# A fifth channel tile of a Conformer convolution moves from TensorE to taps on ScalarE and GpSimd

## The chip, the cores and the metric

The kernel runs on one core of a Trainium2 chip. The metric is the device time of one execution in microseconds. Times come from repeated runs; engine times, waits and order come from one profiled execution.

## The reference

A decoder trunk of two layers over 512 positions of 1024 channels. Layer 0 mixes tokens with a gated DeltaNet, layer 1 with a Conformer convolution; each layer then attends to a fixed memory and applies a squared-ReLU MLP. The change lies in the Conformer module:

```python
def conformer_conv(h, w_pw1, b_pw1, w_dw, b_dw, ln_g, ln_b, w_pw2, b_pw2):
    u = h @ w_pw1 + b_pw1
    u = u[..., :D_MODEL] * jax.nn.sigmoid(u[..., D_MODEL:])
    c = causal_depthwise_conv(u, w_dw) + b_dw       # width 31
    c = jax.nn.silu(layer_norm(c, ln_g, ln_b))      # over the channels
    return c @ w_pw2 + b_pw2
```

Everything is float32. A full-precision product is made of three matmuls of split operands (high by high, low by high, high by low).

## The kernel before

Activations lie channel by position: eight tiles of 128 channels x 512 positions. A weight half of 128 x 1024 is loaded by SP's queue (`raw`), ScalarE casts it to the high part (`wh`, L207), and VectorE or GpSimd subtracts to get the low part (`wl`, L70 by way of the helper `tt`); three halves are held ahead (`NW = 3`). For the first pointwise weight GpSimd makes all low parts, for layer 1's K and V weights every second one. Instructions are written in one order; a planner then orders each engine's queue by what is ready in its own costs, so that the order on an engine can differ from the written one.

The Conformer (`conformer`) walks through 32 positions (`CONV_SEQ`): 0 to 15 are pointwise products (two for each channel tile: value and gate, `pw_mm`, 24 matmuls each), 16 to 31 are the K and V products of the next cross-attention (`kv_unit(1, u)`), which need nothing of the Conformer and fill TensorE. The evacuation `pw_ev(m)` of tile m waits for both products and for `norm.rb`, the row scale that `norm.stat` and `norm.spread` make: VectorE scales the gate (`sg`) and the value (`pa`), ScalarE applies the sigmoid, and VectorE multiplies the two (`x` or `glu`).

Positions are held in four phases (position 4t + s stands in block s). Two ways of convolving follow:

- Tiles 0 to 3 (`m < NDVE`) by taps: `dve_conv` gives a list of 31 taps; the first is a ScalarE product into PSUM (`ca`, L1038), the other 30 are VectorE multiply-adds on that PSUM tile (L73), and ScalarE copies the end to SBUF (L1044). `taps_dve` puts some of the waiting taps into the written order after each position, `TAP_RATE` per microsecond given. `turn(m)` (`"d"` in `CONV_AFTER`) then transposes the tile on TensorE (`cvT`, L1055), so that positions become rows.
- Tiles 4 to 7 on TensorE: 16 DMAs regroup the tile (`xg`), nine DMAs bring its matrices of taps (`taps(m)`, `"t"`), and `conv(m, js)` (`"c"`) makes 72 matmuls whose output already has positions as rows (`cv`, L1071 and L1074).

Either way four VectorE additions per tile add the row block to `Y`, into which the convolution's bias had been loaded, and four `bn_stats` take its statistics. When all eight tiles are in, `ln()` (`"l"`) normalises `Y` (eight VectorE instructions, L79), and `ln_out(m)` (`"o"`) transposes each channel tile back (`lnT`, L1102), applies scale, bias and SiLU on ScalarE and splits the result (`lsh`, `lsl`) for the second pointwise weight. `CONV_AFTER` sets by hand after which position each of these steps is written. All SBUF tiles of 128 x 512 come out of one set of 69 slots; PSUM has eight tiles.

The first layer's short convolutions use both forms as well: `conv_taps` makes a product on ScalarE (`cvq`, L458) and adds it on GpSimd (`cva`, L70) for the first of its taps where it is told to.

Of the kernel before, what the change touches and what calls it, by code (L numbers as in the profile page):

```python
# [21 lines left out]
_VECS = ["dn_norm", "cv_norm", "xa_norm0", "xa_norm1", "xa_mem0", "xa_mem1", "mlp_norm0", "mlp_norm1",  # L22
         "ln_g", "ln_b", "b_pw2"]
OFF = {n: 8 * i for i, n in enumerate(_VECS)}
# [5 lines left out]
OFF["w_tap"] = _o  # L30
_o += NDVE * 31
OFF["out_norm"] = _o
# [6 lines left out]
def tile_trunk(ctx, tc, xT, memT, prm_d, adt_d, bdw_d, tap_d, fin_d, w_ab, w_kq, w_v, w_z, w_dno, w_pw1, w_pw2,  # L39
# [41 lines left out]
    def c4(t):  # L81
        return t.rearrange("p (c i) -> p c i", c=4)
# [901 lines left out]
    def taps(m):  # L984

        TAPS[m] = []
        for i in range(9):
            t = slot(s="tap")
            nc.sync.dma_start(out=t, in_=tap_d[m - NDVE, i])
            TAPS[m].append(t)  # L990

    def conformer(norm, hres, nxt):
# [4 lines left out]
        for y in Y:  # L997
            for i in range(2):
                nc.sync.dma_start(out=y[i], in_=bdw_d[i * 512:(i + 1) * 512].partition_broadcast(P))

# [4 lines left out]
        def pw_ev(m):  # L1005
# [4 lines left out]
            tt(dve, a, st.pop((m, 0)), norm.rb, ALU.mult)  # L1010
            if m < NDVE:
                x7 = fsp.tile([P, 1024], F32, tag="fs", name=nm("x7"))[:, 0:1008].rearrange("p (q t) -> p q t", q=7)
                pool.memset(x7[:, :, 0:10], 0.0)
                stt(x7[:, 3:7, 8:136], c4(a), pc("b_pw1", m), c4(sg), ALU.add, ALU.mult)
                act.copy(x7[:, 0:3, 9:137], x7[:, 4:7, 8:136])
                todo.extend(dve_conv(m, x7))
                return
# [10 lines left out]

        todo, acc = [], {}

        def dve_conv(m, x7):

            def tap(d):
                w, u, e = pc("w_tap", m * 31 + 30 - d), d // 4, d % 4
                src = x7[:, 3 - e:7 - e, 8 - u:136 - u]
                if d == 0:
                    st["ca"] = psum("ca")
                    act.activation(c4(st["ca"]), src, AF.Copy, scale=w)  # L1038
# [13 lines left out]
        def turn(m):  # L1052
# [4 lines left out]
            for r in range(4):  # L1057
                y = Y[r][m // 4][:, m % 4 * P:m % 4 * P + P]
                tt(dve, y, ps[:, r * P:(r + 1) * P], y, ALU.add)
                dve.bn_stats(out=bn[:, (r * 8 + m) * 6:(r * 8 + m) * 6 + 6], in_=y)  # L1060
# [221 lines left out]
    h = xattn(0, n1, h, n2)  # L1282
    n3 = Norm("cv_norm", deng=pool)
    h = mlp(0, n2, h, n3, lambda: (mem_gain(1, 0), mem_gain(1, 1), taps(NDVE)))
    n4 = Norm("xa_norm1")
# [14 lines left out]
    def finish(hid, cur):  # L1300
# [3 lines left out]
        for c, g in LAST:  # L1304
# [14 lines left out]
            if g == 0:  # L1319
# [69 lines left out]
def _taps(np, w):  # L1389
# [11 lines left out]
    e = np.concatenate([e[:, :, :, 0:8].reshape(128, 8, 128), e[:, :, :, 8].reshape(128, 8, 16)], axis=2)  # L1401
    e = e.reshape(4, 32, 8, 9, 16)[:, :, NDVE:]
    t = np.zeros((8 - NDVE, 9, 4, 32, 16, 32), w.dtype)
    for c in range(32):
        t[:, :, :, c, :, c] = e[:, c].transpose(1, 2, 0, 3)
    return t.reshape(8 - NDVE, 9, 128, 512)


def _layout(np, i):
# [3 lines left out]
    def vec(v):  # L1413
# [6 lines left out]
            i["xa_mem_norm"][1], i["mlp_norm"][0], i["mlp_norm"][1], i["cv_ln_g"][0],  # L1420
            i["cv_ln_b"][0], i["cv_b_pw2"][0], i["cv_b_pw1"][0]]
    cols = [vec(v) for v in vecs]
    cols.append(i["dn_w_conv"][0].T.reshape(24, 128, 4).transpose(1, 0, 2).reshape(128, 96))
    cols.append(i["cv_w_dw"][0].T.reshape(8, 128, 31)[:NDVE].transpose(1, 0, 2).reshape(128, NDVE * 31))
    cols.append(i["dn_out_norm"][0].reshape(128, 1))
# [39 lines left out]
```

## Time and profile before

| | |
|---|---|
| runs (three) | 1562.58, 1564.87, 1565.54 us; median 1564.87 |
| profiled execution | 1567.44 us, span 1565.7 us, mean granted clock 0.987 |
| Conformer, first pointwise matmul to second pointwise weight | 868.5 to 1046.8 us of the span |

Engines are PE (TensorE), PEld (its weight loads), DVE (VectorE), ACT (ScalarE), POOL (GpSimd) and SP (the DMA queue). A row of the timeline has the start and length in us, the engine, the line, the operation and the tiles as output<-input; in square brackets stands how long the engine had been idle and what released it. A group has the count, its busy time, the mean of one in ns and the idle time before them. A stretch has its bounds, its length, the busy time and count of each engine, the granted share of TensorE's clock, and the DMA engines' share and GB/s. Matmuls overlap: one of 512 columns is shown as 0.39 us, while the next one starts 0.23 us after it.

### The profile page before, as it was taken

What the parts mean: (1) busy time and instruction counts of PE and PEld (TensorE: products, weight loads), DVE (VectorE), ACT (ScalarE), POOL (GpSimd) and SP (SyncE); (2) the same over time, 40 slices, a digit from 0 to 9 for tenths busy, and PEclk for the clock granted to TensorE, in tenths of its full rate; (3) what the DMA queues carried; (4) which work ended last, traced back from release to release, by engine and by line L of the source; (5) the groups of instructions that cost most, each with busy time, mean ns of one, the idle gap of its engine ahead of it and who ended that gap; (6) DMA issues with size and microseconds to landing.
All of it is one profiled execution on the core that took longest, in us unless ns stands there. A gap on an engine that the chain in (4) does not pass through costs nothing.

```text
span 1565.7 us, 19421 instructions
## 1 busy us (share of the span) xinstructions
PE 1530.1 (98%) x7630; PEld 1289.4 (82%) x7630; DVE 903.2 (58%) x1372; ACT 653.3 (42%) x1017; POOL 186.6 (12%) x202
## 2 busy tenths in 40 slices
PE   8999996999999999999999999999999999999998
PEld 6887885988888888888888889978888888888886
DVE  6798788666655444343435499874545443434441
ACT  5855656454544443231424332264434442323332
POOL 1221122101212000000002441112112000000000
PEclk9999998899999999999999999999999999999999
DMA  5222122252222222233224624443213223322231
GB/s 169 66 81 68 55 68 87 85 179 75 87 68 68 94 95 94 96 104 97 95 94 154 207 87 152 167 137 106 69 40 108 94 95 95 102 99 95 94 108 54
DMA packets 51115, 156.17 MB, mean 100 GB/s; under 512 B 6608, under 2 KB 8912, under 8 KB 51024
## 3 DMA queue, kind: packets, MB, share of 16 engines
q1 hardware_dynamic: 51024, 154.93, 30.4%
q8 instruction: 60, 0.98, 0.3%
q14 instruction: 31, 0.25, 0.0%
HBM read 151.76 MB, written 2.10 MB: 98 GB/s over the span
## 4 chain that ended last, share of the span: by engine, by line
PE 89%; DVE 6%; ACT 1%; issue 1%; DMA 1%; SPq 1%; POOL 0%; ACTq 0%; POOLq 0%; DVEq 0%
PE up L229 7%; PE up L230 7%; PE up L231 7%; PE dn L230 6%; PE dn L229 6%; PE dn L231 6%; PE pw L229 3%; PE pw L231 3%; PE pw L230 3%; PE q L229 2%; PE xo L230 2%; PE q L230 2%; PE xo L231 2%; PE q L231 2%; PE xo L229 2%; PE h L230 1%
## 5 line engine op out<-in xcount | busy, mean ns | idle before, releaser
L207 ACT CAST wh<-raw 128x1024 fp32r<-128x1024 f32 x248 | 260.3, 1051 | 675.3 <-PE dn L230 194.8
L70 DVE TENSOR_TENSOR wl<-raw,wh 128x1024 fp32r<-128x1024 f32 x224 | 277.4, 1239 | 96.5 <-ACT wh L207 94.9
L229 PE MATMUL up<-xh,wh 128*128 128x512 f32 x512 | 200.3, 391 | 0.0
L231 PE MATMUL up<-xh,wl 128*128 128x512 f32 x512 | 199.3, 389 | 0.0
L230 PE MATMUL up<-xl,wh 128*128 128x512 f32 x512 | 199.3, 389 | 0.0
L231 PE MATMUL dn<-uh,wl 128*128 128x512 f32 x448 | 174.4, 389 | 0.0
L230 PE MATMUL dn<-ul,wh 128*128 128x512 f32 x448 | 174.4, 389 | 0.0
L229 PE MATMUL dn<-uh,wh 128*128 128x512 f32 x448 | 174.4, 389 | 0.0
L70 DVE TENSOR_TENSOR h<-dn,h 128x512 f32<-128x512 f32 x56 | 41.8, 747 | 163.3 <-PE dn L231 163.3
L73 DVE SCALAR_TENSOR_TENSOR rl<-up,rb 128x512 f32<-128x512 f32 x64 | 44.2, 690 | 157.0 <-PE up L231 157.0
L229 PEld LDWEIGHTS up<-xh,wh 128*128 128x128 f32 x512 | 96.1, 188 | 20.3 <-issue 0.5
L230 PEld LDWEIGHTS up<-xl,wh 128*128 128x128 f32 x512 | 96.2, 188 | 20.2 <-issue 0.5
L231 PEld LDWEIGHTS up<-xh,wl 128*128 128x128 f32 x512 | 96.1, 188 | 20.0
L70 POOL TENSOR_TENSOR sq<-sq,sq 128x512 f32<-128x512 f32 x30 | 47.8, 1592 | 465.0 <-ACT sq L304 465.0
L229 PEld LDWEIGHTS dn<-uh,wh 128*128 128x128 f32 x448 | 84.1, 188 | 17.5
L231 PEld LDWEIGHTS dn<-uh,wl 128*128 128x128 f32 x448 | 84.1, 188 | 17.4
L230 PEld LDWEIGHTS dn<-ul,wh 128*128 128x128 f32 x448 | 84.1, 188 | 17.4
L73 DVE SCALAR_TENSOR_TENSOR ca<-x,prm,ca 128x512 f32<-128x512 f32 x120 | 87.8, 748 | 3.0 <-ACT ca L1038 1.2
L229 PE MATMUL h<-xh,wh 128*128 128x512 f32 x192 | 78.7, 410 | 3.1 <-ACT xh L297 3.1
L230 PE MATMUL h<-xl,wh 128*128 128x512 f32 x192 | 76.5, 398 | 0.6 <-DVE xl L73 0.6
L231 PE MATMUL h<-xh,wl 128*128 128x512 f32 x192 | 76.1, 397 | 0.0
L70 POOL TENSOR_TENSOR wl<-raw,wh 128x1024 fp32r<-128x1024 f32 x24 | 57.6, 2407 | 114.5 <-ACT wh L207 107.4
(334 smaller groups left out, 3034.3 us busy)
## 6 DMA issues: line engine op xcount, KB each, us to landing
raw<-w_up SPq DMA_DIRECT2D x64, 512.0 KB, 3.6
raw<-w_dn SPq DMA_DIRECT2D x64, 512.0 KB, 3.6
raw<-w_pw SPq DMA_DIRECT2D x24, 512.0 KB, 3.7
tap<-tap SPq DMA_DIRECT2D x36, 256.0 KB, 5.4
raw<-w_kq SPq DMA_DIRECT2D x16, 512.0 KB, 3.6
raw<-w_k SPq DMA_DIRECT2D x16, 512.0 KB, 3.8
raw<-w_vv SPq DMA_DIRECT2D x16, 512.0 KB, 3.7
raw<-w_q SPq DMA_DIRECT2D x16, 512.0 KB, 3.6
```

The costliest lines, as they stand in the source:

```text
L70: return e.tensor_tensor(out=o, in0=a, in1=b, op=op)
L73: dve.scalar_tensor_tensor(out=o, in0=a, scalar=s, in1=b, op0=op0, op1=op1)
L207: ins = [act.copy(h, raw)]
L229: pe.matmul(ps, wh, xh, start=first, stop=False)
L230: pe.matmul(ps, wh, xl, start=False, stop=False)
L231: pe.matmul(ps, wl, xh, start=False, stop=last)
```

## The change

Tile 4 is no longer convolved by TensorE, and five tiles (`NTAP = 5`) go by taps. Tiles 1 to 4 keep `dve_conv`. Tile 0 goes by a new function, `pool_conv`: ScalarE makes each tap's product in SBUF (in two pieces where the tap crosses a phase) and GpSimd adds it to the sum; `taps_pool` places two taps per pointwise position, one per K or V position, and three after a convolution. The bias enters with the first tap (Identity with a bias in place of Copy), so a turned tile is not added to `Y`: ScalarE copies the transposed block to `Y` and VectorE takes its statistics straight from PSUM. Only the half of `Y` for tiles 4 to 7 is still loaded with the bias. The row scale is spread after the second product in place of the third, its diagonal is made by VectorE instead of GpSimd, and tile 0 is evacuated there. The steps of `CONV_AFTER` are placed anew: the matrices of tiles 6 and 7 are loaded after positions 3 and 13, and tile 0 is turned after position 20.

```diff
-NDVE = 4
+NTAP = 5
...
         for y in Y:
-            for i in range(2):
-                nc.sync.dma_start(out=y[i], in_=bdw_d[i * 512:(i + 1) * 512].partition_broadcast(P))
+            nc.sync.dma_start(out=y[1], in_=bdw_d[512:1024].partition_broadcast(P))
...
-            if m < NDVE:
+            if m == 0:
+                x4 = c4(wp.tile([P, 544], F32, tag="cv", name=nm("xp"), bufs=NCV))
+                pool.memset(x4[:, :, 0:8], 0.0)
+                stt(x4[:, :, 8:136], c4(a), pc("b_pw1", m), c4(sg), ALU.add, ALU.mult)
+                todo_p.extend(pool_conv(m, x4))
+                return
+            if m < NTAP:
...
+        def pool_conv(m, x4):
+            a = acc[m] = slot(s="ca")
+
+            def tap(d):
+                w, u, e = pc("w_tap", m * 31 + 30 - d), d // 4, d % 4
+                if d == 0:
+                    act.activation(c4(a), x4[:, :, 8:136], AF.Identity, scale=w, bias=pc("b_dw", m))
+                    return
+                b = slot(s="cvp")
+                act.activation(c4(b)[:, e:4], x4[:, 0:4 - e, 8 - u:136 - u], AF.Copy, scale=w)
+                if e:
+                    act.activation(c4(b)[:, 0:e], x4[:, 4 - e:4, 7 - u:135 - u], AF.Copy, scale=w)
+                tt(pool, a, a, b, ALU.add)
+
+            return [lambda d=d: tap(d) for d in range(31)]
...
-                    act.activation(c4(st["ca"]), src, AF.Copy, scale=w)
+                    act.activation(c4(st["ca"]), src, AF.Identity, scale=w, bias=pc("b_dw", m))
...
+        def taps_pool(n):
+            for _ in range(min(len(todo_p), n)):
+                todo_p.pop(0)()
...
-                y = Y[r][m // 4][:, m % 4 * P:m % 4 * P + P]
-                tt(dve, y, ps[:, r * P:(r + 1) * P], y, ALU.add)
+                y = ps[:, r * P:(r + 1) * P]
+                act.copy(Y[r][m // 4][:, m % 4 * P:m % 4 * P + P], y)
                 dve.bn_stats(out=bn[:, (r * 8 + m) * 6:(r * 8 + m) * 6 + 6], in_=y)
...
-                if (m, hf) == (1, 0):
+                if (m, hf) == (0, 1):
                     norm.spread()
-                    pw_ev(0)
-                if hf == 1 and m > 0:
+                if hf == 1:
                     pw_ev(m)
...
             taps_dve(5.4 if kind == "p" else 2.8)
+            taps_pool(2 if kind == "p" else 1)
...
                 taps_dve({"c": 2.0 * len(js)}.get(what, 0.0))
+                taps_pool(3 if what == "c" else 0)
...
-    n3 = Norm("cv_norm", deng=pool)
+    n3 = Norm("cv_norm")
...
-CONV_AFTER = [(3, ("t", 5)), (11, ("d", 0)), (12, ("c", 4, 0, 1)), (13, ("c", 4, 2, 3)), (13, ("t", 6)),
-              (14, ("c", 5, 0, 1, 2, 3)), (14, ("t", 7)), (15, ("d", 1)), (16, ("c", 6, 0, 1, 2, 3)), (18, ("d", 2)),
-              (18, ("c", 7, 0, 1, 2, 3)), (23, ("d", 3)), (23, ("l", 0))]
+CONV_AFTER = [(3, ("t", 6)), (9, ("d", 1)), (13, ("d", 2)), (13, ("c", 5, 0, 1, 2, 3)), (13, ("t", 7)),
+              (16, ("c", 6, 0, 1, 2, 3)), (17, ("d", 3)), (18, ("c", 7, 0, 1, 2, 3)), (20, ("d", 0)), (23, ("d", 4)),
+              (23, ("l", 0))]
```

The host side packs the convolution's bias and the fifth tile's taps into the parameter tile, and the tap matrices of three tiles instead of four.

More of the change, by code (lines that the diff above doesn't have):

```diff
@@ L22 @@
 _VECS = ["dn_norm", "cv_norm", "xa_norm0", "xa_norm1", "xa_mem0", "xa_mem1", "mlp_norm0", "mlp_norm1",
-         "ln_g", "ln_b", "b_pw2"]
+         "ln_g", "ln_b", "b_pw2", "b_dw"]
 OFF = {n: 8 * i for i, n in enumerate(_VECS)}
@@ L30 @@
 OFF["w_tap"] = _o
-_o += NDVE * 31
+_o += NTAP * 31
 OFF["out_norm"] = _o
@@ L988, in taps @@
             t = slot(s="tap")
-            nc.sync.dma_start(out=t, in_=tap_d[m - NDVE, i])
+            nc.sync.dma_start(out=t, in_=tap_d[m - NTAP, i])
             TAPS[m].append(t)
@@ L1027, in pw_ev @@
             xg[m] = x4
-        todo, acc = [], {}
+        todo, todo_p, acc = [], [], {}
+        def pool_conv(m, x4):
[11 more added lines that the diff above has]
+            return [lambda d=d: tap(d) for d in range(31)]
         def dve_conv(m, x7):
@@ L1282, in tile_trunk @@
     h = xattn(0, n1, h, n2)
-    n3 = Norm("cv_norm", deng=pool)
-    h = mlp(0, n2, h, n3, lambda: (mem_gain(1, 0), mem_gain(1, 1), taps(NDVE)))
+    n3 = Norm("cv_norm")
+    h = mlp(0, n2, h, n3, lambda: (mem_gain(1, 0), mem_gain(1, 1), taps(NTAP)))
     n4 = Norm("xa_norm1")
@@ L1401, in _taps @@
     e = np.concatenate([e[:, :, :, 0:8].reshape(128, 8, 128), e[:, :, :, 8].reshape(128, 8, 16)], axis=2)
-    e = e.reshape(4, 32, 8, 9, 16)[:, :, NDVE:]
-    t = np.zeros((8 - NDVE, 9, 4, 32, 16, 32), w.dtype)
+    e = e.reshape(4, 32, 8, 9, 16)[:, :, NTAP:]
+    t = np.zeros((8 - NTAP, 9, 4, 32, 16, 32), w.dtype)
     for c in range(32):
         t[:, :, :, c, :, c] = e[:, c].transpose(1, 2, 0, 3)
-    return t.reshape(8 - NDVE, 9, 128, 512)
+    return t.reshape(8 - NTAP, 9, 128, 512)
 def _layout(np, i):
@@ L1420, in _layout @@
             i["xa_mem_norm"][1], i["mlp_norm"][0], i["mlp_norm"][1], i["cv_ln_g"][0],
-            i["cv_ln_b"][0], i["cv_b_pw2"][0], i["cv_b_pw1"][0]]
+            i["cv_ln_b"][0], i["cv_b_pw2"][0], i["cv_b_dw"][0], i["cv_b_pw1"][0]]
     cols = [vec(v) for v in vecs]
     cols.append(i["dn_w_conv"][0].T.reshape(24, 128, 4).transpose(1, 0, 2).reshape(128, 96))
-    cols.append(i["cv_w_dw"][0].T.reshape(8, 128, 31)[:NDVE].transpose(1, 0, 2).reshape(128, NDVE * 31))
+    cols.append(i["cv_w_dw"][0].T.reshape(8, 128, 31)[:NTAP].transpose(1, 0, 2).reshape(128, NTAP * 31))
     cols.append(i["dn_out_norm"][0].reshape(128, 1))
```

## The prediction

> **What bounds the kernel now.** I read the page first, then the busy time by stretches, then the queues of VectorE and TensorE in order of time around the Conformer.
>
> ```profile
> span 1565.7 us, 19421 instructions
> ...
> PE 1530.1 (98%) x7630; PEld 1289.4 (82%) x7630; DVE 903.2 (58%) x1372; ACT 653.3 (42%) x1017; POOL 186.6 (12%) x202
> ```
>
> TensorE is busy for 98% of the span, so over the whole kernel less matmul work is less time. But the change touches one stage, and there the shares differ. The next four rows cut that stage: pointwise products, convolution with K products, the wait for LayerNorm, and the rest up to the second pointwise weight (length; busy time of PE, PEld, DVE, ACT, POOL; granted clock; DMA share).
>
> ```profile
> 868.50:974.00 105.50, 105.50 (x543) 89.75 (x542) 86.79 (x141) 30.34 (x38) 36.99 (x17) 1.00 0.44 143
> 974.00:1024.80 50.80, 49.66 (x386) 47.41 (x384) 45.39 (x94) 16.99 (x20) 13.29 (x6) 1.00 0.55 186
> 1024.80:1028.90 4.10, 1.50 (x8) 0.65 (x6) 4.10 (x7) 2.33 (x2) 1.33 (x1) 0.97 0.62 218
> 1028.90:1046.80 17.90, 17.90 (x88) 14.85 (x88) 10.22 (x13) 13.55 (x19) 2.40 (x1) 0.91 0.43 129
> ```
>
> VectorE is nearly full from its first evacuation to 1028.9, and in the third stretch TensorE waits for it:
>
> ```profile
> 1024.77 0.27 PE L1102 MATMUL lnT<-ident,cy 128*128 128x128 f32 x1
> ...
> 1026.93 0.33 PE L1102 MATMUL lnT<-ident,cy 128*128 128x128 f32 x1 [1.89 <-DVE cy L79]
> ...
> 1027.93 0.48 PE L260 MATMUL V<-wh,mh 128*128 128x512 f32 x1
> ...
> 1028.76 0.47 PE L1102 MATMUL lnT<-ident,cy 128*128 128x128 f32 x1
> ...
> 1029.45 0.63 PE L260 MATMUL V<-wh,mh 128*128 128x512 f32 x1
> ...
> 1031.59 0.62 PE L262 MATMUL V<-wh,ml 128*128 128x512 f32 x1
> ```
> ```profile
> 886.20:935.60 49.40, 49.40 (x216) 1.00 0.41 138
> ```
>
> The first transpose of the normalised rows stands at 1024.77, the fourth at 1028.76. Of these 4.0 us some 3.3 are waiting; the rest is the transposes and two V matmuls put between them. After the wait V matmuls start 0.43 us apart (five steps from 1029.45 to 1031.59), where pointwise matmuls of the same width take 49.40 / 216 = 0.23 (the last row, their busy time alone): about eight of them, 1.6 us more, at a granted clock of 0.91 in the stretch. So in this stage TensorE is ahead of VectorE by under 4 us, and VectorE sets when LayerNorm ends.
>
> **The change, part by part.** *TensorE.* Tile 4's convolution leaves, and a turned tile's four transposes come instead.
>
> ```profile
> 960.50:968.50 8.00, 7.98 (x72) 1.00 0.21 63
> ...
> 935.74 0.44 PE cvT L1055 x4
> ...
> 1033.10:1035.90 2.80, 2.80 (x12) 1.00 0.07 28
> ```
>
> The first row is one tile's convolution alone, the second one tile's transposes: 7.98 - 0.44 = 7.5 us less TensorE work. The third is one V unit, 2.80 us; one pointwise product (24 matmuls) is 49.4 / 9 = 5.49 us.
>
> *VectorE begins later.* It still multiplies four tiles, but now tiles 1 to 4.
>
> ```profile
> 885.74 1.02 PE L325 MATMUL rb<-dg,ones 128*128 128x512 f32 x2
> ...
> 887.42 0.69 DVE L70 TENSOR_TENSOR sg<-pw,rb 128x512 f32<-128x512 f32 x1 [12.06 <-ACT rb L327]
> ...
> 891.38 7.09 DVE L73 SCALAR_TENSOR_TENSOR ca<-x,prm,ca 128x512 f32<-128x512 f32 x9 [1.17 <-ACT ca L1038]
> ```
>
> Before, tile 0 is evacuated behind the third product, at 887.42. The scale's spread moves ahead of the third product, so tile 0 follows the second, at about 881.9, while tile 1, the first for VectorE, needs the fourth: 885.74 + 0.45 + 5.49 = 891.7. Taps follow an evacuation after 891.38 - 887.42 = 3.96 us, of which a table load that tile 0 now pays takes 0.6; first tap 895.1, that is 3.7 later. The diagonal of the scale moves from GpSimd to VectorE, into the 12.06 us of idle time shown: nothing.
>
> *VectorE's work after its first tap.*
>
> ```profile
> L73 DVE SCALAR_TENSOR_TENSOR ca<-x,prm,ca 128x512 f32<-128x512 f32 x120 | 87.8, 748 | 3.0 <-ACT ca L1038 1.2
> ...
> L70 DVE TENSOR_TENSOR cy<-cv,cy 128x128 f32<-128x128 f32 x16 | 4.1, 278 | 3.9 <-PE cv L1074 3.9
> ...
> L70 DVE TENSOR_TENSOR cy<-cvT,cy 128x128 f32<-128x128 f32 x16 | 4.1, 274 | 0.0
> ...
> L73 DVE SCALAR_TENSOR_TENSOR glu<-pa,prm,sg 128x512 f32<-128x512 f32 x4 | 3.0, 746 | 0.3 <-DVE bn L1082 0.3
> ...
> L70 DVE TENSOR_TENSOR sg<-pw,rb 128x512 f32<-128x512 f32 x8 | 5.5, 684 | 12.1 <-ACT rb L327 12.1
> ...
> 942.60 0.28 DVE L70 TENSOR_TENSOR cy<-cvT,cy 128x128 f32<-128x128 f32 x1
> 942.80 0.74 DVE L73 SCALAR_TENSOR_TENSOR ca<-x,prm,ca 128x512 f32<-128x512 f32 x1
> ```
>
> The 120 taps stay. One evacuation fewer lies behind the first tap: two readings of PSUM at 0.68 and a product at 0.75, less their overlap, 2.0 us. The bias additions of turned tiles go: 5 tiles x 4 = 20, since tile 4 had four as well; the next instruction starts 0.20 after one (942.60 to 942.80): 4.0 us, at most 20 x 0.28 = 5.6. The statistics are as many; that they now read PSUM I put at nothing, since readings of PSUM (0.68) are not longer than the product of two SBUF tiles (0.75). VectorE's 3.9 us of waiting for convolutions (the second row) may partly go, with 7.5 us less ahead of them and 9 tap loads, 16 regroupings and 4 bias broadcasts fewer on SP's queue; the loads for tiles 6 and 7 also move forward to positions 3 and 13, where those of 5 and 6 stood. Between 0 and 3.9, I take 2.
>
> *GpSimd and ScalarE.* Thirty sums come to GpSimd, next to the weight halves that it makes for TensorE.
>
> ```profile
> L70 POOL TENSOR_TENSOR wl<-raw,wh 128x1024 fp32r<-128x1024 f32 x10 | 23.9, 2401 | 28.2 <-ACT wh L207 28.2
> ...
> L70 POOL TENSOR_TENSOR cva<-cva,cvq x12: 1266/1286/1734, 57.6 to 282.3; 128x512 f32<-128x512 f32 x12
> ...
> L1013 POOL MEMSET x<- 128x70 f32 x1 | 0.2, 158 | 3.4 <-DVE ca L73 3.4
> ...
> L458 ACT ACTIVATE cvq<-cv,prm 128x512 f32<-128x512 f32 x12 | 8.6, 720 | 0.0
> ...
> L1015 ACT COPY x<-x 128x384 f32<-128x384 f32 x4 | 2.1, 517 | 3.9 <-DVE x L73 3.9
> ...
> L1008 ACT ACT_TABLE_LOAD x1 | 1.3, 1283 | 0.0
> ...
> L595 ACT COPY y<-mg 64x128 f32<-64x128 f32 x8 | 1.9, 255 | 3.6 <-PE mg L592 3.5
> ...
> ACT sg L1008 <- DVE sg L70: 24.8, 6, 6.0
> ```
>
> The same pair exists in the first layer: a product at 0.72 us, a sum at 1.29. In each pointwise step GpSimd now does 2.40 + 2 x 1.29 = 4.98 of 5.49 us, 91%. The fill of the fourth VectorE tile's margin, which waits 3.4 us for the first one's last tap (three buffers), stays, now with sums and weight halves behind it. The sums are over by about position 14 and tile 0 is turned at position 20, so their own end is covered. ScalarE: 7 whole products x 0.72, 23 pairs between 0.517 + 0.255 = 0.77 and 2 x 0.72 (0.9 taken, nearer to the parts), one first tap, and 20 row copies at about 0.26: 5.0 + 20.7 + 0.7 + 5.2 = 32 us, beside some 50 of the first three stretches' 160. That fits; if it did not, weight halves would be late (below). Identity in place of Copy I put at no table load; the upper bound is ten more loads of 1.28, 12.8 us for which ScalarE has the room. [...]
>
> *The shared access.* One thing comes back to VectorE.
>
> ```profile
> 858.73 2.39 POOL L70 TENSOR_TENSOR wl<-raw,wh 128x1024 fp32r<-128x1024 f32 x1 [2.35 <-ACT wh L207]
> ...
> 859.66 2.02 DVE L73 SCALAR_TENSOR_TENSOR xl<-h,prm,xh 128x512 fp32r<-128x512 f32 x1 [0.79 <-ACT xh L297]
> ...
> 1055.40 0.74 DVE L73 SCALAR_TENSOR_TENSOR xl<-h,prm,xh 128x512 fp32r<-128x512 f32 x1
> ```
>
> An instruction of VectorE with two SBUF tensors takes 2.02 us beside a weight half on GpSimd and 0.74 alone: it ends 0.56 after GpSimd has. [...]
>
> Taps have one input in PSUM: their mean of 748 ns covers many beside a weight half. What can collide is the last product of an evacuation, six times (tiles 1 to 6). It finds a weight half with 2.40 / 5.49 = 0.44 and waits 1.2 on average, a sum with 0.47 and waits 0.65: 0.83 x 6 = 5.0 us. Bounds: 0, if the order keeps them apart as now (0.745 each), and 6 x (2.02 - 0.74) = 7.7.
>
> *Sum for LayerNorm's end.* +3.7 - 2.0 - 4.0 - 2.0 + 5.0 = +0.7 us; bounds 3.7 - 2.0 - 5.6 - 3.9 + 0 = -7.8 and 3.7 - 2.0 - 4.0 + 7.7 = +5.4. So VectorE ends where it did.
>
> *What follows it.* The stretch of 17.9 us after LayerNorm holds the V units at positions 27 to 31 less two matmuls, 5 x 2.80 - 0.47 = 13.5 us, that need nothing of it. TensorE now comes to the transposes 7.5 us earlier. Its queue is not in written order: the planner puts work that is ready in front of work that waits, as the V products between the transposes at 1026.93 and 1028.76 show. With 7.5 us more lead it will put one to three V units there; I take two, 5.6 us; bounds none and all 13.5, though TensorE's own work stops the whole at -12.4 (the last rival). TensorE waits longer, but pays the slow products once as before. Sum: +0.7 - 5.6 = **-4.9 us**. The profiled execution's 1567.4 (span 1565.7 and 1.7 around it) would become 1562.5; the median of the runs is 2.57 lower, so the forecast is 1564.9 - 4.9 = **1560.0 us**.
>
> **Rivals.** *Slower: GpSimd becomes the bound of the pointwise phase.* A sum waits for its product, the product stands on ScalarE behind a sigmoid that waits for VectorE (six such waits, 24.8 us, 4.1 each), and the next weight half stands behind the sum. Per tile GpSimd needs 9.96 of 10.98 us; 4.1 us with nothing to do leave it 3.1 late, in six tiles 18.6. TensorE alone could come 7.5 + 3.3 + 1.6 = 12.4 earlier, so the end is 6.2 later: 1571.1. It decides from 3.1 us of such idle time per tile on. Against it: three weights are held ahead, and lateness of TensorE shortens VectorE's own lag.
>
> *No change: VectorE alone counts.* If no V unit is put ahead, only the +0.7 is left: 1565.6. For it stands the position written for the first transpose, unchanged; against it the V products seen between.
>
> *More gain: TensorE becomes the only bound.* If collisions are rare and V units enough, -7.5 - 4.9 = -12.4: 1552.5. For it: 98% on the page; against it VectorE's late first tap.
>
> **How the numbers follow.** Forecast 0.48, slower 0.25, no change 0.15, more gain 0.12. A measurement of this kernel can tell 0.2%, 3.1 us, from no change. Of the forecast's 0.48, 0.42 lies under -3.1 and 0.06 within; the no-change case is 0.11 within and 0.04 above (its bound is +5.4), and of the slow case 0.02 stays within. Faster 0.54, same 0.19, slower 0.27. The range leaves out the last of each side: 1552 to 1570; the forecast's own is 1556 to 1563.
>
> **What would show it.** Right: first VectorE tap near 895; 216 instead of 288 convolution matmuls; 12 bias additions; GpSimd over 80% busy from 890 to 950; V units ahead of the first LayerNorm transpose; LayerNorm's end within 3 us of 1029. Wrong: TensorE waits for weight halves from GpSimd in the pointwise products (the slow rival); the x and glu products at 0.75 (no collisions, more gain); transposes still right behind the third V unit (no change).

## The result, and the profile after

The changed kernel is slower: a median of 1569.84 us (seven runs, 1567.55 to 1572.17) against 1564.87 (seven runs, 1562.58 to 1567.54), a ratio of 1.0034 [1.0022, 1.0046]. The forecast was 1560.0, faster by 4.9 us; it is slower by 5.0.

The page of the changed kernel:

```profile
span 1565.8 us, 19357 instructions
...
PE 1520.2 (97%) x7562; PEld 1280.4 (82%) x7562; DVE 907.6 (58%) x1353; ACT 680.6 (43%) x1091; POOL 226.9 (14%) x231
```

TensorE is busy for 9.9 us less, as intended, and yet the time grew. The span is no guide here, for two reasons: the profiled execution of the changed kernel is the shortest of its seven, and before the Conformer, where both kernels have the same matmuls in the same order, the granted clock was low at different times. Two stretches of 20 us of both, after and then before (columns: bounds, length; busy time and count of PE, PEld, DVE, ACT, POOL; granted clock; DMA share, GB/s):

```profile
130.00:150.00 20.00, 17.53 (x144) 14.86 (x143) 19.11 (x30) 11.04 (x23) 1.05 (x6) 1.00 0.32 106
272.00:292.00 20.00, 20.00 (x144) 19.64 (x144) 14.77 (x18) 13.17 (x22) 2.77 (x4) 0.82 0.16 53
```
```profile
130.00:150.00 20.00, 17.52 (x110) 15.35 (x109) 17.59 (x27) 11.86 (x23) 1.05 (x6) 0.83 0.26 80
272.00:292.00 20.00, 16.32 (x101) 15.97 (x102) 10.35 (x11) 11.49 (x17) 6.22 (x7) 0.69 0.22 69
```

In the first, the same busy time of 17.5 us held 144 matmuls at a granted clock of 1.00 and 110 at 0.83. A `dt` matmul ahead of it (L440) stands at 53.72 after and 54.69 before, an `h` matmul within it (L230) at 140.77 and 144.74. The Conformer begins at 863.8 instead of 868.5. So I measure the **stage**: from the first pointwise matmul to the first matmul of the second pointwise weight. The whole stage, before and then after:

```profile
868.50:1046.80 178.30, 174.56 (x1020) 152.67 (x1018) 146.49 (x251) 63.21 (x79) 54.01 (x24) 0.99 0.48 155
```
```profile
863.80:1047.10 183.30, 168.71 (x952) 147.58 (x950) 150.87 (x232) 90.90 (x153) 93.90 (x53) 0.96 0.41 131
```

The stage is 5.0 us longer, as much as the medians differ. TensorE's busy time fell by 174.56 - 168.71 = 5.85 us; its idle time, length less busy time, rose from 3.74 to 14.59, by 10.85. Where the idle time lies, by stretches of the changed kernel and by TensorE's queue:

```profile
863.80:912.00 48.20, 48.20 (x216) 39.69 (x215) 30.05 (x37) 26.30 (x42) 33.96 (x20) 1.00 0.52 154
912.00:956.00 44.00, 34.11 (x154) 28.24 (x152) 42.46 (x64) 24.98 (x51) 35.57 (x23) 0.91 0.33 104
956.00:1014.60 58.60, 58.60 (x452) 56.69 (x452) 55.10 (x96) 16.88 (x29) 15.92 (x9) 0.98 0.36 121
1014.60:1029.90 15.30, 10.60 (x44) 8.52 (x43) 12.99 (x26) 7.28 (x12) 4.25 (x2) 0.89 0.33 103
1029.90:1047.10 17.20, 17.20 (x94) 14.45 (x92) 10.28 (x12) 15.46 (x21) 4.20 (x2) 1.00 0.57 195
```
```profile
922.42 0.66 PE L1080 MATMUL cvT<-ident,ca 128*128 128x128 f32 x4 [2.24 <-ACT ca L1065]
...
952.53 1.12 PE L1080 MATMUL cvT<-ident,ca 128*128 128x128 f32 x4 [7.66 <-ACT ca L1065]
...
1019.61 0.87 PE L1080 MATMUL cvT<-ident,ca 128*128 128x128 f32 x4 [4.70 <-ACT ca L1065]
...
1029.90 0.60 PE L1127 MATMUL lnT<-ident,cy 128*128 128x128 f32 x4
1030.25 0.48 PE L260 MATMUL V<-wh,mh 128*128 128x512 f32 x1
```

All of it lies in front of three turns: 2.24 + 7.66 + 4.70 = 14.60 us. `ca` is the copy of a tap tile out of PSUM, so TensorE waits there for VectorE's taps of tiles 1, 2 and 4. A turn stands in TensorE's queue ahead of products that need nothing of it, and these stood still with it. Before the change no turn made TensorE wait. In front of the transposes back (`lnT`), where the prediction had put the wait, there is none now; the first comes behind three V units, as written, and nothing was put ahead.

VectorE is late because it starts late:

```profile
887.58 0.69 DVE L70 TENSOR_TENSOR sg<-pw,rb 128x512 f32<-128x512 f32 x1 [7.48 <-PE pw L231]
...
889.73 1.75 DVE L73 SCALAR_TENSOR_TENSOR x<-pa,prm,sg 128x512 f32<-128x512 f32 x1 [0.86 <-ACT sg L1007]
892.75 3.92 DVE L73 SCALAR_TENSOR_TENSOR ca<-x,prm,ca 128x512 f32<-128x512 f32 x5 [1.26 <-ACT ca L1059]
...
1024.55 3.74 DVE L79 TENSOR_SCALAR cy<-cy,mv,lrs 128x512 f32<-128x512 f32 x8
```

Tile 0 is evacuated, and then VectorE waits 7.48 us for tile 1's second product. The "first tap" is the start of the first `ca` row. From here on, times are counted from the stage's start. The first VectorE tap stands at 892.75 - 863.8 = 28.9, against 22.9 before: 6.07 later. LayerNorm ends at 1028.29 - 863.8 = 164.5, against 160.7: 3.83 later. From there to the stage's end it is 18.8 us, against 17.6. So the 5.0 us add up from 6.07 for the start, -2.24 for what follows up to LayerNorm's end, and 1.17 behind it; that is a sum of measured times, and which of them causes which is for the runs to show.

### The profile page after: what moved, and what is told of

Read it like the earlier page. It is cut to its first block, busy times and chain, and to the rows that moved or that the text cites. A ratio compares the mean times of both kernels' runs of the same rounds, so it can differ in the third digit from the quotient of the medians.

```text
span 1565.8 us, 19357 instructions
## 1 busy us (share of the span) xinstructions
PE 1520.2 (97%) x7562; PEld 1280.4 (82%) x7562; DVE 907.6 (58%) x1353; ACT 680.6 (43%) x1091; POOL 226.9 (14%) x231
## 3 DMA queue, kind: packets, MB, share of 16 engines
q1 hardware_dynamic: 48384, 151.28, 28.9%
## 4 chain that ended last, share of the span: by engine, by line
PE 87%; DVE 9%; ACT 2%; issue 1%; POOL 0%; DMA 0%; SPq 0%; ACTq 0%; DVEq 0%; POOLq 0%
PE up L229 7%; PE up L230 7%; PE up L231 7%; PE dn L230 6%; PE dn L229 6%; PE dn L231 6%; DVE ca L73 3%; PE pw L229 2%; PE pw L230 2%; PE pw L231 2%; PE q L229 2%; PE xo L230 2%; PE q L230 2%; PE q L231 2%; PE xo L231 2%; PE xo L229 2%
## 5 line engine op out<-in xcount | busy, mean ns | idle before, releaser
L230 PE MATMUL up<-xl,wh 128*128 128x512 f32 x512 | 199.2, 389 | 0.0
L230 PE MATMUL dn<-ul,wh 128*128 128x512 f32 x448 | 174.3, 389 | 0.0
L230 PEld LDWEIGHTS up<-xl,wh 128*128 128x128 f32 x512 | 96.1, 188 | 20.3 <-issue 0.5
L229 PEld LDWEIGHTS dn<-uh,wh 128*128 128x128 f32 x448 | 84.1, 188 | 17.5
L231 PEld LDWEIGHTS dn<-uh,wl 128*128 128x128 f32 x448 | 84.1, 188 | 17.5
L230 PEld LDWEIGHTS dn<-ul,wh 128*128 128x128 f32 x448 | 84.1, 188 | 17.4
L230 PE MATMUL h<-xl,wh 128*128 128x512 f32 x192 | 75.8, 395 | 0.9 <-DVE xl L73 0.9
```

Of the source, the lines that this page charges most:

```text
L229: pe.matmul(ps, wh, xh, start=first, stop=False)
L230: pe.matmul(ps, wh, xl, start=False, stop=False)
L231: pe.matmul(ps, wl, xh, start=False, stop=last)
```

## The experiments

The theory (A): VectorE's four tiles became tiles 1 to 4, so their taps are late by a product, and the waits in front of the turns are that lateness. Rivals: the turns are merely written too early in TensorE's queue (B), or GpSimd's sums hold up VectorE or ScalarE (C). All runs in one table; ratios are against runs of the kernel before on the same chip as each, and the last five columns, in us, come from one profiled execution each. "Idle" is the stage's length less TensorE's busy time. Against the kernel before, the change of the stage in a single profile and that of the median differ by 3.1 us in last_turn_late and by up to 1.6 in the others, so smaller differences between two rows decide nothing by themselves.

| run | median us | ratio | stage | idle | first tap | last turn | LayerNorm's end |
|---|---|---|---|---|---|---|---|
| before | 1564.87 | | 178.3 | 3.7 | 22.9 | 147.6 | 160.7 |
| after | 1569.84 | 1.0034 [1.0022, 1.0046] | 183.3 | 14.6 | 28.9 | 155.8 | 164.5 |
| turns_late | 1566.24 | 1.0016 [1.0005, 1.0027] | 180.4 | 12.2 | 28.9 | 152.4 | 161.3 |
| last_turn_late | 1564.26 | 0.9997 [0.9988, 1.0007] | 176.3 | 10.4 | 28.9 | 157.9 | 169.0 |
| tile1_gpsimd | 1556.12 | 0.9958 [0.9944, 0.9973] | 170.3 | 4.7 | 17.5 | 141.6 | 157.0 |
| no_sums | 1568.07 | 1.0031 [1.0020, 1.0042] | 182.2 | 13.5 | 28.9 | 153.5 | 162.5 |
| late_taps | 1568.53 | 1.0023 [1.0011, 1.0036] | 181.7 | 6.5 | 28.9 | 151.0 | 165.6 |
| early_start | 1563.98 | 0.9994 [0.9984, 1.0005] | 177.1 | 3.3 | 17.5 | 145.6 | 159.5 |
| bias_only | 1558.26 | 0.9967 [0.9954, 0.9979] | 173.4 | 1.1 | 23.0 | 146.7 | 160.0 |
| bias_early | 1560.43 | 0.9969 [0.9957, 0.9982] | 172.2 | 0.6 | 17.6 | 145.6 | 158.9 |
| three_tiles | 1562.55 | 0.9990 [0.9981, 1.0000] | 177.1 | 3.9 | 28.9 | 142.6 | 158.1 |
| tile1_last | 1558.10 | 0.9965 [0.9946, 0.9983] | 172.5 | 5.5 | 17.6 | 147.3 | 160.7 |
| tile1_back_late | 1557.59 | 0.9955 [0.9941, 0.9969] | 171.9 | 6.2 | 17.6 | 142.6 | 160.1 |
| tile1_conv_late | 1554.99 | 0.9942 [0.9926, 0.9957] | 169.9 | 3.9 | 17.6 | 143.0 | 156.5 |

### Is it the place of the turns? turns_late and last_turn_late

turns_late, against the changed kernel: turns later, nothing else.

```diff
-CONV_AFTER = [(3, ("t", 6)), (9, ("d", 1)), (13, ("d", 2)), (13, ("c", 5, 0, 1, 2, 3)), (13, ("t", 7)),
-              (16, ("c", 6, 0, 1, 2, 3)), (17, ("d", 3)), (18, ("c", 7, 0, 1, 2, 3)), (20, ("d", 0)), (23, ("d", 4)),
+CONV_AFTER = [(3, ("t", 6)), (12, ("d", 1)), (13, ("c", 5, 0, 1, 2, 3)), (13, ("t", 7)),
+              (16, ("d", 2)), (16, ("c", 6, 0, 1, 2, 3)), (18, ("c", 7, 0, 1, 2, 3)), (18, ("d", 3)), (20, ("d", 0)),
```

> Edit: only the written places of three turns move back (tile 1 from position 9 to 12, tile 2 from 13 to 16 behind the convolution of tile 5, tile 3 from 17 to 18); no work changes. Measure: the stage from the first pointwise matmul to the first matmul of the second pointwise weight, 178.3 us before and 183.3 us after the change. Theory A (VectorE's stream of taps sets the end of the stage, TensorE's waits at the turns are only where its lead is spent): the 2.4 and 7.8 us waits at the first two turns vanish but come back as later waits, stage 182 to 184, time within 2 us of the change. Theory B (TensorE's queue: the turns stand too early in it, and the work behind them is held up for good): stage about 173 to 175, time 8 to 10 us under the change. Theory C (GpSimd's sums slow VectorE and the weight halves): no difference from the change.

TensorE's waits in the stage:

```profile
PE K L231 <- DVE wl L70: 5.3, 1, 5.3
PE cvT L1080 <- ACT ca L1065: 4.5, 1, 4.5
PE cv L1096 <- DMA xg<-glu: 2.4, 3, 1.6
```

The first two waits for taps are gone, and 5.3 us of waiting for a weight half, which VectorE makes behind its taps, stand in their place. The idle time falls by 2.4 us and the stage by 2.9. The stage of 180.4 lies in neither range: under the 182 to 184 of A, and far above the 173 to 175 of B. So VectorE is late and TensorE pays most of it in one place or another: A is the nearer one, and the places of these three turns are worth the 2.9 us.

last_turn_late moves the last turn and LayerNorm from position 23 to 26, and the transposes back to the end:

```diff
-              (16, ("c", 6, 0, 1, 2, 3)), (17, ("d", 3)), (18, ("c", 7, 0, 1, 2, 3)), (20, ("d", 0)), (23, ("d", 4)),
-              (23, ("l", 0))]
-CONV_AFTER += [(_i, ("o", _m)) for _m, _i in enumerate((26, 27, 28, 29, 30, 30, 31, 31))]
+              (16, ("c", 6, 0, 1, 2, 3)), (17, ("d", 3)), (18, ("c", 7, 0, 1, 2, 3)), (20, ("d", 0)), (26, ("d", 4)),
+              (26, ("l", 0))]
+CONV_AFTER += [(_i, ("o", _m)) for _m, _i in enumerate((29, 29, 30, 30, 31, 31, 31, 31))]
```

> Edit: the turn of tile 4 and LayerNorm are written after position 26 instead of 23, and the transposes back after 29 to 31, so that three more V units and some of the later ones stand ahead of them in TensorE's queue. No work changes. Theory A: VectorE's last tap and LayerNorm's end stay (164.4 us after the stage's start), but what TensorE has left behind it shrinks from five V units to about two, so ScalarE's eight pairs of 1.4 us limit: stage 175 to 178, time 5 to 8 us under the change. Theory B: the 5.0 us wait and the slow products behind it (1.4) go: stage about 177, the same; the two differ in where LayerNorm ends (A: within 1 us of 164.4; B: earlier). Theory C: 183.

The stage came out as expected, LayerNorm's end did not: it ends 4.5 us later than in the changed kernel, because the V work now ahead of it takes VectorE and ScalarE too. The stage is 7.0 shorter all the same: V work done ahead of LayerNorm need not follow it. The wait of the last turn has gone; the earlier two stay (9.8 us). The two theories were to part at LayerNorm's end, and it moved the way of neither, so this run does not decide between them. It shows that place counts for more than A allowed: with the late start kept, the time is that of the kernel before (0.9997 [0.9988, 1.0007]).

### Is it the late start? tile1_gpsimd and late_taps

tile1_gpsimd gives GpSimd tile 1 in place of tile 0, so that VectorE takes tiles 0, 2, 3, 4 and can begin with tile 0:

```diff
-            if m == 0:
+            if m == 1:
...
-CONV_AFTER = [(3, ("t", 6)), (9, ("d", 1)), (13, ("d", 2)), (13, ("c", 5, 0, 1, 2, 3)), (13, ("t", 7)),
-              (16, ("c", 6, 0, 1, 2, 3)), (17, ("d", 3)), (18, ("c", 7, 0, 1, 2, 3)), (20, ("d", 0)), (23, ("d", 4)),
+CONV_AFTER = [(3, ("t", 6)), (9, ("d", 0)), (13, ("d", 2)), (13, ("c", 5, 0, 1, 2, 3)), (13, ("t", 7)),
+              (16, ("c", 6, 0, 1, 2, 3)), (17, ("d", 3)), (18, ("c", 7, 0, 1, 2, 3)), (20, ("d", 1)), (23, ("d", 4)),
```

> Edit: tile 1 instead of tile 0 goes to ScalarE and GpSimd, so that VectorE can begin its taps with tile 0, two pointwise products earlier; the turns of tiles 0 and 1 change places. Theory A: VectorE's first tap comes 5 to 8 us earlier than in the change (28.9 us after the stage's start), LayerNorm's end moves forward by about as much less one more evacuation (2 us): 3 to 6 us, stage 176 to 180. Theory B: the turns still stand where they stood, stage within 2 us of 183.3. Theory C: within 2 us of 183.3, as the sums are as many.

Its pointwise groups on TensorE, VectorE's first taps, and waits of TensorE:

```profile
L229 PE MATMUL pw<-xh,wh x128: 389/389/793, 865.1 to 964.7; 128*128 128x512 f32 x128
...
L229 PE MATMUL pw<-lsh,wh x64: 389/389/476, 1035.4 to 1078.4; 128*128 128x512 f32 x64
```
```profile
882.62 11.84 DVE L73 SCALAR_TENSOR_TENSOR ca<-x,prm,ca 128x512 f32<-128x512 f32 x15 [1.26 <-ACT ca L1059]
```
```profile
PE cv L1096 <- DMA xg<-glu: 2.3, 5, 0.8
PE lnT L1127 <- DVE cy L79: 1.6, 1, 1.6
PE V L261 <- DVE wl L70: 0.7, 1, 0.7
```

VectorE's first tap stands at 17.5, where it stood at 28.9, and no turn waits. The stage, 1035.4 - 865.1 = 170.3 us, is 13.0 shorter than with the change as it is, more than expected (176 to 180), from one number of a tile and the two turns that go with it. The same GpSimd sums, the same positions for turns, and as much TensorE work are in both.

late_taps does the reverse: the kernel before, with only the roles exchanged, so that VectorE takes tiles 1 to 4 and TensorE tile 0. There is no GpSimd tile, and the other edits only make the indices of taps and tap matrices follow (left out here).

```diff
-            if m < NDVE:
+            if 1 <= m <= NDVE:
...
-CONV_AFTER = [(3, ("t", 5)), (11, ("d", 0)), (12, ("c", 4, 0, 1)), (13, ("c", 4, 2, 3)), (13, ("t", 6)),
-              (14, ("c", 5, 0, 1, 2, 3)), (14, ("t", 7)), (15, ("d", 1)), (16, ("c", 6, 0, 1, 2, 3)), (18, ("d", 2)),
-              (18, ("c", 7, 0, 1, 2, 3)), (23, ("d", 3)), (23, ("l", 0))]
+CONV_AFTER = [(3, ("t", 5)), (11, ("d", 1)), (12, ("c", 0, 0, 1)), (13, ("c", 0, 2, 3)), (13, ("t", 6)),
+              (14, ("c", 5, 0, 1, 2, 3)), (14, ("t", 7)), (15, ("d", 2)), (16, ("c", 6, 0, 1, 2, 3)), (18, ("d", 3)),
+              (18, ("c", 7, 0, 1, 2, 3)), (23, ("d", 4)), (23, ("l", 0))]
```

> Edit: the kernel before with only the roles of tiles changed: TensorE convolves tiles 0, 5, 6, 7 and VectorE tiles 1 to 4 (before: 4 to 7 and 0 to 3). Work on every engine is the same, nothing goes to GpSimd, and the turns are written where they stood. Theory A (VectorE's late start is the loss): first tap 28 to 29 us after the stage's start in place of 22.9, last turn later than 147.7 by 3 to 8 us, TensorE waits at its turns, stage 181 to 186 (178.3 before), time 3 to 8 us over before. Rival F (the loss came from the route over ScalarE and GpSimd or from the new places of the turns): stage within 1 us of 178.3.

```profile
895.08 2.34 DVE L73 SCALAR_TENSOR_TENSOR ca<-x,prm,ca 128x512 f32<-128x512 f32 x3 [1.17 <-ACT ca L1038]
```
```profile
1017.16 1.11 PE L1055 MATMUL cvT<-ident,ca 128*128 128x128 f32 x4 [4.06 <-ACT ca L1044]
```

The stage began at 866.2, so the first tap is at 28.9 as in the changed kernel. A wait for the last turn appears, 4.06 us, LayerNorm ends 4.9 later, and the stage is 3.4 us longer than before. The late start alone makes the kernel slower, without anything else of the change. So that it costs is shown from both sides; that it is not the only way to the loss or out of it, last_turn_late shows.

### Is it GpSimd? no_sums

29 of the 30 sums go:

```diff
-                tt(pool, a, a, b, ALU.add)
+                if d == 30:
+                    tt(pool, a, a, b, ALU.add)
```

> Edit: 29 of the 30 sums of tile 0 on GpSimd are left out (its convolution is then not complete); ScalarE's products stay. Theory A: VectorE's products x and glu no longer meet GpSimd's sums (three of them took 1.00, 2.39 and 1.65 and one x 1.75 us instead of 0.75), so LayerNorm ends 2 to 4 us earlier, stage 179 to 181. Theory B: stage 183, the turns still wait. Theory C: GpSimd is the main cost: stage 175 or less, at least 8 us under the change.

```profile
PE cvT L1081 <- ACT ca L1066: 13.5, 3, 6.6
```

With GpSimd's busy time back from 93.9 to 54.7 us, three turns still wait 13.5 us, and the stage is 1.1 us shorter. That is less than A said (179 to 181), and B had said 183 with waiting turns, so this run speaks against C alone: C, and with it the prediction's slower rival, falls.

### What the other parts are worth: early_start, bias_only, bias_early, three_tiles

early_start is the kernel before with the early spread of the scale alone; bias_only the kernel before with the bias in the first tap and turned tiles only read; bias_early has both. None has a fifth tap tile. (Where the bias is in the first tap, half of `Y`'s bias loads go with it, as in the change; left out here.)

```diff
-                if (m, hf) == (1, 0):
+                if (m, hf) == (0, 1):
                     norm.spread()
-                    pw_ev(0)
-                if hf == 1 and m > 0:
+                if hf == 1:
...
-    n3 = Norm("cv_norm", deng=pool)
+    n3 = Norm("cv_norm")
```
```diff
-                    act.activation(c4(st["ca"]), src, AF.Copy, scale=w)
+                    act.activation(c4(st["ca"]), src, AF.Identity, scale=w, bias=pc("b_dw", m))
...
-                y = Y[r][m // 4][:, m % 4 * P:m % 4 * P + P]
-                tt(dve, y, ps[:, r * P:(r + 1) * P], y, ALU.add)
+                y = ps[:, r * P:(r + 1) * P]
+                act.copy(Y[r][m // 4][:, m % 4 * P:m % 4 * P + P], y)
```

> Edit: the kernel before, with one small part of the change alone: the row scale is spread after the second pointwise product (its diagonal made by VectorE) and tile 0 is evacuated there. Tile 4 stays on TensorE, the bias stays in Y. Theory A (VectorE's stream sets the end, so what counts is when it starts and how much it has): first tap 5.3 us earlier (17.6 us after the stage's start in place of 22.9), LayerNorm ends 3 to 5 us earlier, TensorE's wait of 3.3 us ahead of the transposes goes and then TensorE limits: stage 173 to 175 (178.3 before), time 3 to 5 us under before. Rival D (the gain of the kernel with tile 1 on GpSimd came from the 7.5 us less work on TensorE): stage within 1 us of 178.3.

> Edit: the kernel before, with another part of the change alone: the bias in the first tap of tiles 0 to 3, turned tiles copied to Y by ScalarE and read by VectorE's statistics straight from PSUM, half of Y's bias loads gone. Theory A: 16 additions of 0.2 us fewer on VectorE, LayerNorm ends 2 to 3 us earlier, stage 175 to 176.5, time 2 to 3 us under before. Rival D: stage within 1 us of 178.3.

> Edit: the kernel before with the bias in the first tap (as in bias_only) and the early spread of the row scale (as in early_start), four tiles by VectorE, four by TensorE, nothing on GpSimd. Against the kernel with tile 1 on GpSimd this differs by the fifth tile alone (7.2 us less TensorE work there). If the fifth tile is worth its work once VectorE begins in time: 171 to 174, above the 170.3 of that kernel. If it is worth nothing: 169 to 171, time as that kernel's. If the two small parts were worth nothing together: 176 to 178.

early_start missed: the first tap comes 5.4 us earlier, the last turn 2.1 and the stage 1.2. In the kernel before, the last turn follows TensorE's K products directly, so its taps were ready; an earlier start seems to have little to give there, while a later one costs at once (late_taps). bias_only gives more than expected. With VectorE's additions gone the planner now puts 40 V matmuls ahead of the first transpose back and others between them, and the wait there is short:

```profile
PE lnT L1121 <- DVE cy L79: 0.6, 1, 0.6
```

That is the kind of filling which the prediction expected of the whole change, but smaller: 48 V matmuls stand ahead of the fourth transpose, where 38 did before, and a V unit has 12. bias_early adds 1.2 us of stage to it; by the time the two are alike. TensorE is idle for 0.6 us of its stage. By time, bias_only alone is 5.6 us faster than before (1563.83 on the same chip, 1558.26), and its interval overlaps that of tile1_gpsimd: how much of that kernel's gain comes from the fifth tile is not shown by time.

three_tiles keeps GpSimd's tile 0 and leaves VectorE tiles 1 to 3; TensorE convolves four tiles, as before.

```diff
-NTAP = 5
+NTAP = 4
...
+CONV_AFTER = [(3, ("t", 5)), (10, ("d", 1)), (12, ("c", 4, 0, 1)), (13, ("c", 4, 2, 3)), (13, ("t", 6)),
+              (14, ("d", 2)), (14, ("c", 5, 0, 1, 2, 3)), (14, ("t", 7)), (16, ("c", 6, 0, 1, 2, 3)), (18, ("d", 3)),
+              (18, ("c", 7, 0, 1, 2, 3)), (20, ("d", 0)), (23, ("l", 0))]
```

> Edit: the changed kernel with tile 4 back on TensorE: tile 0 by ScalarE and GpSimd, tiles 1 to 3 by VectorE, tiles 4 to 7 by TensorE. VectorE still begins late, but with 30 taps (about 21 us) and one turned tile fewer; TensorE has 7.5 us more than in the change. Theory A: VectorE is no longer the bound, TensorE does not wait for its turns, stage 171 to 174 (TensorE's own work is about 170), time 4 to 7 us under before. Rival D: stage 183.3 + 7.5 = about 190.

```profile
PE cv L1099 <- DMA tap<-tap: 3.9, 1, 3.9
```

No turn waits, since VectorE has 30 taps fewer, and LayerNorm ends 2.6 us earlier than before; but the stage is only 1.2 us shorter than before, at 177.1 (171 to 174 expected). 3.9 us of it is a wait for a tap matrix's DMA, and the transposes back again follow three V units as written. So the late start stops costing once VectorE has a tile less, and this run does not tell more.

### Can the rest be had? tile1_last, tile1_back_late, tile1_conv_late

All three are tile1_gpsimd with other positions: the last turn, LayerNorm and transposes back later; the transposes back alone; the convolutions on TensorE later. Each edit is shortened to what differs from tile1_gpsimd.

```diff
-(23, ("d", 4)), (23, ("l", 0))
+(25, ("d", 4)), (25, ("l", 0))
-enumerate((26, 27, 28, 29, 30, 30, 31, 31))
+enumerate((28, 28, 29, 29, 30, 30, 31, 31))
```
```diff
-enumerate((26, 27, 28, 29, 30, 30, 31, 31))
+enumerate((28, 28, 29, 29, 30, 30, 31, 31))
```
```diff
-(13, ("c", 5, 0, 1, 2, 3)), (13, ("t", 7))
+(14, ("c", 5, 0, 1, 2, 3)), (14, ("t", 7))
-(16, ("c", 6, 0, 1, 2, 3))
+(17, ("c", 6, 0, 1, 2, 3))
-(18, ("c", 7, 0, 1, 2, 3))
+(20, ("c", 7, 0, 1, 2, 3))
```

> Edit: the kernel with tile 1 on GpSimd, and also the turn of tile 4 and LayerNorm written after position 25, the transposes back after 28 to 31. No work changes. Theory A: LayerNorm ends where it did (157.0 us after the stage's start) or 1 to 3 us later because of V work put ahead; TensorE has about two V units fewer left behind it: stage 166 to 170 (170.3 without the edit), time 6 to 11 us under before. Rival D: 170.3, as TensorE's work is the same.

> Edit: the kernel with tile 1 on GpSimd, and only the transposes after LayerNorm are written later (after 28 to 31 instead of 26 to 31), so that all five V units of the second half stand ahead of the first of them; the last turn and LayerNorm stay at 23. Theory A: LayerNorm's end stays at 157 within 1 us, TensorE's 2.2 us of waiting ahead of and in the transposes goes, but ScalarE's eight pairs (1.4 us each) then follow each other: stage 168 to 170.5 (170.3 without the edit). Rival: putting V work ahead also puts its ScalarE and VectorE work ahead of LayerNorm, as in the kernel whose LayerNorm was written later: stage 172 or more.

> Edit: the kernel with tile 1 on GpSimd, and the convolutions of tiles 5, 6 and 7 written after positions 14, 17 and 20 instead of 13, 16 and 18. No work changes. In the kernel without this edit TensorE waits 4 us in all for the regrouped tiles of 5 and 7 (seven steps of 0.3 to 1.1 us between groups of convolution matmuls), because it now comes to them earlier than their DMAs. Theory A (TensorE has the lead again and loses it only to waits that better places avoid): these waits fall to 1 us or less, stage 166.5 to 168.5 (170.3 without the edit), time 9 to 12 us under before. Rival: VectorE is again the bound there and the wait reappears at the last turn or ahead of the transposes: 169.5 to 171.

The first two missed: LayerNorm ends 3.7 and 3.1 us later than in tile1_gpsimd, probably because V work put ahead of it also needs VectorE and ScalarE, and the stage is 2.2 and 1.6 longer; by time, their intervals overlap that of tile1_gpsimd. The third gains 0.4 us of stage and lies in the range of its rival: of the waits for regrouping DMAs (2.3 us) 1.0 is left, but a weight half of VectorE's is late instead.

```profile
PE K L231 <- DVE wl L70: 2.1, 1, 2.1
PE cv L1096 <- DMA xg<-glu: 1.0, 1, 1.0
PE lnT L1127 <- DVE cy L79: 0.7, 1, 0.7
```

It is the best version found, 1554.99 us, 0.9942 [0.9926, 0.9957] of the kernel before; its interval overlaps that of tile1_gpsimd. Against bias_early, which has no fifth tile, its stage is 2.3 us shorter, though TensorE is busy for 171.60 - 166.05 = 5.5 us less: 3.3 us went into these waits. Whether another order keeps them as well stays open. By time, the two intervals only touch ([0.9926, 0.9957] and [0.9957, 0.9982]), so that the fifth tile pays is likely, not more.

## Why the prediction was wrong, step by step

- **TensorE's saving** was right in kind and a little large: 7.5 was said, busy time fell by 5.85. Between two kernels whose granted clock was 1.00 over the stage, bias_early and tile1_gpsimd, it is 171.60 - 165.62 = 6.0; where the other 1.5 us are was not followed up. The convolution has 216 matmuls, as said.
- **VectorE's start** is the term that was mis-sized: +3.7 said, +6.07 measured. Tile 1's evacuation came 4.9 us later relative to the stage (4.3 said). From it to the first tap it took 5.17 us, where 3.4 was said: the `sg` of tile 1 stood behind one of ScalarE's new products, and the `x` product took 1.75 us beside a weight half on GpSimd. The table load (1.28 us on ScalarE) was gone from there, but that product stood in its place.
- **VectorE's work behind it** was near in sum, partly by luck: -2.0 - 4.0 - 2.0 + 5.0 = -3.0 said, -2.2 measured. Groups of VectorE between first tap and LayerNorm's end in the changed kernel, and the whole of that stretch, before and then after:

```profile
L73 DVE SCALAR_TENSOR_TENSOR ca<-x,prm,ca 128x512 f32<-128x512 f32 x120 | 88.4, 750 | 3.4 <-ACT ca L1059 1.3
...
L73 DVE SCALAR_TENSOR_TENSOR glu<-pa,prm,sg 128x512 f32<-128x512 f32 x3 | 5.0, 1682 | 0.0
...
L79 DVE TENSOR_SCALAR cy<-cy,mv,lrs 128x512 f32<-128x512 f32 x8 | 3.7, 544 | 0.0
L70 DVE TENSOR_TENSOR cy<-cv,cy 128x128 f32<-128x128 f32 x12 | 2.9, 282 | 1.6 <-PE cv L1099 1.6
```
```profile
891.38:1029.16 137.78, 134.04 (x831) 119.37 (x830) 130.66 (x233) 40.35 (x48) 41.01 (x18) 1.00 0.46 154
892.75:1028.29 135.54, 120.95 (x723) 108.11 (x722) 127.95 (x209) 59.62 (x108) 70.76 (x42) 0.95 0.38 126
```

  Twelve additions remain, and taps are as before. Their wait for convolutions fell from 3.9 to 1.6, but VectorE's idle time in the stretch did not fall (137.78 - 130.66 = 7.1 before, 135.54 - 127.95 = 7.6 after): other waits came. Collisions: three `glu` at 1.682 instead of 0.745 make 2.8 us, where 5.0 was said for this and the `x` products; the `x` product that took 1.75 lies ahead of the first tap and is in the start. The 5.0 was an estimate from two `xl` rows of the kernel before (2.02 us beside a weight half, 0.74 alone), which show none beside a sum; in the changed kernel one `glu` took 1.00 us beside the end of a sum and the start of a weight half, the others 2.39 and 1.65 beside weight halves. The eight LayerNorm instructions took 3.74 us instead of 5.80, which no term of the sum had. LayerNorm's end is +3.8, inside the bound of +5.4, where +0.7 was taken.
- **GpSimd and ScalarE** were right: from 880 to 965 GpSimd makes 30 sums (39.5 us) and 12 weight halves (29.6), 81% of the time, TensorE waits for none of its weight halves in the pointwise products, and ScalarE's busy time on the page rose by 680.6 - 653.3 = 27.3 us, where 32 was taken. Identity added no table load, as the prediction had assumed: three of 1.28 us stand in the stage before, and three after.
- **What follows LayerNorm** is the step that failed. It said that TensorE would come to the transposes 7.5 us earlier, wait there, and find two V units put ahead, -5.6; measured, the part behind LayerNorm's end is +1.17. Of the 9.9 us between forecast and result this makes 6.8, the later LayerNorm 3.1. In the run TensorE had spent its lead before: 14.6 us in front of three turns, which the prediction had costed at 0.44 us of transposes each. The positions in the diff were at hand: three turns moved forward (11, 15, 18 to 9, 13, 17) while their taps began later, and TensorE ran nothing of its queue in those 14.6 us. Then no V unit was put ahead. That the planner does so because in its costs VectorE is on time is read from the code, not tested; some filling did come where no turn waited (bias_only, tile1_gpsimd). That V work ahead was worth its time is shown by last_turn_late: there 72 V matmuls stand ahead of the first transpose back instead of 36, because they are written there, and the stage is 7.0 us shorter, though LayerNorm ends later.
- **The rivals.** The slower one had the sign by a mechanism that no_sums refutes. "VectorE alone counts" came nearest: no V unit ahead, and a later LayerNorm; its +0.7 carried the same mis-sized start.

## What to carry to other kernels

When a transpose or a copy-out of another engine's result is moved, cost it by the time at which that result is ready, at its new place in the waiting engine's queue, and not by its own length: here 14.6 us against 1.3. When an engine that feeds the end of a stage takes other tiles, look which tile it can start with; giving GpSimd tile 1 instead of tile 0 turned 5.0 us lost into 7.1 won (1563.18 before on the same chip, 1556.12), most of which the bias in the first tap brings alone (5.6 in bias_only). A wait that vanishes when its instruction is moved is not yet time gained: in turns_late it came back as a wait for a weight half.

## What the runs showed of the hardware beyond that

- Behind some waits of TensorE the granted clock was lower, behind others it was not. In the changed kernel, behind its waits of 2.24, 7.66 and 4.70 us:

```profile
922.40:928.00 5.60, 5.58 (x27) 4.69 (x28) 5.20 (x10) 5.24 (x12) 4.61 (x3) 1.00 0.16 60
952.50:958.50 6.00, 5.97 (x28) 5.97 (x29) 5.85 (x11) 4.28 (x12) 5.02 (x4) 0.50 0.39 135
1019.60:1024.50 4.90, 4.89 (x17) 4.00 (x18) 3.25 (x10) 3.23 (x7) 0.00 (x0) 0.65 0.36 110
```

  The granted clock is 1.00, 0.50 and 0.65. In early_start a wait of 2.56 us, with one of 0.58 behind it, was followed by a clock of 0.72, with V matmuls 0.43 us apart from 1023.56 to 1026.12:

```profile
1020.93 0.33 PE L1102 MATMUL lnT<-ident,cy 128*128 128x128 f32 x1 [2.56 <-DVE cy L79]
...
1020.90:1027.00 6.10, 5.37 (x17) 3.87 (x18) 4.08 (x7) 1.78 (x3) 0.00 (x0) 0.72 0.48 164
```

  In tile1_last it was 0.53 for 3.6 us behind a wait of 2.65, with V matmuls 0.42 to 0.43 us apart from 1024.52 to 1025.80 and 0.23 from 1026.09 on. In the kernel before, behind waits of 1.9 us and less, 3.3 us of them within 4.0, V matmuls started 0.43 us apart as well (the prediction's rows). Behind a wait of 1.55 us in tile1_gpsimd the clock was 1.00. The kernel before, and then tile1_gpsimd:

```profile
1028.80:1032.00 3.20, 3.20 (x8) 2.54 (x9) 2.18 (x3) 1.40 (x2) 0.00 (x0) 0.50 0.25 60
```
```profile
1018.90:1023.50 4.60, 4.58 (x24) 3.62 (x25) 4.29 (x8) 1.97 (x2) 0.86 (x1) 1.00 0.33 121
```

  No run shows what decides between the two, or whether short waits close together add up.
- A VectorE instruction with one SBUF tensor, too, was longer beside a weight half on GpSimd. In the kernel before, one of the eight LayerNorm instructions (L79) took 2.60 us where the others took 0.53 to 0.55; the group's 5.80 us became 3.74 in the changed kernel, where no weight half ran beside it:

```profile
1023.36 5.80 DVE L79 TENSOR_SCALAR cy<-cy,mv,lrs 128x512 f32<-128x512 f32 x8
...
1023.51 2.62 POOL L70 TENSOR_TENSOR wl<-raw,wh 128x1024 fp32r<-128x1024 f32 x1 [3.65 <-ACT wh L207]
```

  The eight took 5.78 us in early_start, 5.88 in late_taps, 5.81 in tile1_last and 6.15 in tile1_back_late as well; in three_tiles two of them took 2.67 where two others took 1.00; in the other runs the eight took 3.74 to 4.09. Why the one was longer, no run shows. Taps, whose accumulator is in PSUM, stayed at 750 ns (748 before) beside 30 more GpSimd sums.
- The same matmuls, in the same order, took 4.7 us more up to the Conformer in the kernel before than in the changed one, with a granted clock of 0.83 against 1.00 and of 0.69 against 0.82 in the two stretches above. With differences of this size a stage has to be compared with a stage.
